# One load of B's sample rows moved to GpSimd's queue, beside two smaller reorderings, in a hybrid decoder step on one core

## The chip, the cores and the metric

The kernel is one program on 1 core of one Trainium2 chip. The metric is the device time of one execution in microseconds (us). A core has five engines that run side by side and meet through semaphores: TensorE (PE in the profile, its weight loads PEld), VectorE (DVE), ScalarE (ACT), GpSimd (POOL) and SyncE (SP), which issues most of the DMAs. ACT and POOL have DMA queues of their own. Each engine takes its instructions strictly in the order of its own program, so an instruction that waits holds all that stand behind it.

## The reference, cut to what matters

One layer of a decoder: 256 new prompt tokens and 8 samples of 8 tokens (320 tokens in all), width 2048, in float32.

```python
def decoder_layer(x, ssm_state, ssm_conv_state, ffn_conv_state, p):
    h = rms_norm(x, p["norm_mix_pre"])
    proj = h @ p["w_in"]                 # [gMLP u | gMLP v | SSD z | SSD x,B,C | dt]
    ...
    gate_out, chunk_v = chunk_spatial_gate(a_u, a_v, ...)     # gelu(u) * (tril(W_s) v_norm + b)
    ssm_out, new_ssm, new_ssm_conv = ssd_mixer(z, xbc, dt_raw, ssm_state, ...)
    mix = jnp.concatenate([gate_out, ssm_out], axis=-1) @ p["w_out"]
    x = x + rms_norm(mix, p["norm_mix_post"])
    f, new_ffn_conv = conv_ffn(rms_norm(x, p["norm_ffn_pre"]), ffn_conv_state, ...)
    return x + rms_norm(f, p["norm_ffn_post"]), new_ssm, new_ssm_conv, new_ffn_conv, chunk_v

# in ssd_mixer: convolution and silu over x, B, C, then for 4 groups of 8 heads
#   h_t = exp(dt_t a) h_{t-1} + dt_t x_t B_t^T,   y_t = h_t C_t
# y = (y + d_skip * x) * silu(z); y is normed over each group of 512 columns; * norm_w
```

The samples bring a recurrent state (8 samples, 32 heads, 64 x 128 each), which is read, decayed, added to and written back.

## The kernel before, in words

**Products.** Every large product is made in three matmuls: a weight slab of 512 KB is loaded in float32 (tile `wraw`, by SP), rounded by ACT (`whi`, line 123), the rest is taken by DVE (`wlo`, line 124), and PE adds high x high, low x high and high x low for all 320 tokens at a time (lines 153 to 155). `wraw`, `whi` and `wlo` have three buffers each, so a load starts when the `wlo` three slabs back is made, and a rounding when PE has left the `whi` three slabs back. One slab is 24 matmuls.

**Stages.** W_in's column blocks and W_out's row blocks take turns: v, B and C (their result for B, turned to rows of tokens, is written to `b_d` in DRAM by `to_tokens`), x of the first head group, four projections of u (`gate_up`), each followed by `gate_mix` and by a part of W_out (`chunk_out`), then the four SSD groups with x, z and W_out's other parts, then the feed-forward layer. The gate stage has its tiles in the pool `gp`, the SSD stage in the pool `sd`, which takes over `gp`'s memory: the first instruction that writes to an `sd` tile waits for the last readers of `gp`.

**Small work between slabs.** `ssd(g)`, `norm()` and others are generators. After each slab a `tick` lets them issue their next step; a `yield 24, 0` asks for 24 matmuls in between. What they issue is then laid into each engine's order by a scheduler that goes by priorities (`first()`, `tc.high_priority`) and by its own times. The order in which the program text issues things is therefore not the order of the engines.

**What the change touches.**
- `b4` (lines 838 to 841): B's 64 sample rows, 32 at a time, each block written four times under one another to 128 partitions. SP loads two tiles of 128 x 512 from `b_d`; the tiles lie in `sd`, under the tags `s1` and `xde`.
- `b_of_samples` (lines 843 to 848): ACT copies `b4` to `bsp` in another column order, rounded; for the partitions 32 to 63 and 96 to 127 DVE takes the rest. `picked` later scales `bsp` to `bm` on ACT.
- `norm` (lines 1136 to 1146): y times its root, four blocks, each split into a high (`ohi`) and a low part (`olo`) for `chunk_out`.
- `shrinks` (line 1054): the step at which GpSimd decays each of a group's pairs of states `st` (line 969).
- The tag `pv` of pool `tp` has four buffers; `scaled` (line 409) puts each block of a gate projection there (`ev`) before ACT's Gelu reads it.

PE's short work of a group, in this order: `xt_ps` (transposes of the samples' x), `s_ps`, then `yo_ps` (line 958), which reads the four pairs of states; the fourth pair, `st3`, is loaded last (line 883). `cs` (line 875) are rows of sums that the decays of the scores need.

Of the kernel before, what the change touches and what calls it, by code (L numbers as in the profile page):

```python
# [8 lines left out]
F32 = mybir.dt.float32  # L9
# [3 lines left out]
ALU = mybir.AluOpType  # L13
# [3 lines left out]
P = 128  # L17
NP = 256
NB, TS = 8, 8
NS = NB * TS  # L20
NT = NP + NS
# [12 lines left out]
def hybrid_step(  # L34
# [10 lines left out]
    act, dve, pool, pe, sp = nc.scalar, nc.vector, nc.gpsimd, nc.tensor, nc.sync  # L45
# [6 lines left out]
    tp = ctx.enter_context(tc.tile_pool(name="tp", bufs=2))  # L52
# [46 lines left out]
    def col(i):  # L99
        return prm[:, i:i + 1]  # L100


    def first():

        return tc.high_priority(offset=200000)
# [60 lines left out]
    def advance(tasks, task):  # L166

        try:
            need = next(task) or (0, 0)
            due[task] = made_so_far[0] + need[0], need[1]  # L170
            return True
        except StopIteration:
            tasks.remove(task)
            return False
# [13 lines left out]
    def finish(task):  # L188
        while task in side:
            advance(side, task)  # L190
        while task in bg:
            advance(bg, bg[0])
# [60 lines left out]
    def chunk_out(w, ck, hi, lo, begins, done=None, rate=1, apart=False):  # L253

        for nb in range(KD):
            if nb % 2 == 0:
                wb = slab(rows_of(w, 4 * ck, 4, P * nb, 256))
            ps = mm.tile([P, 512], F32, tag="mm", name=f"pd_{ck}_{nb}")
            for k in range(4):
                made = accumulate(ps[:, :NT], wb(k, nb % 2), hi[:, k, :], lo[:, k, :], k == 0, k == 3)  # L260
            with first():
                if begins:
                    act.copy(acc[:, nb, :], ps[:, :NT])
                else:
                    for ts in parts_of(nb) if apart else (slice(0, NT),):
                        added_last[:] = [dve.tensor_tensor(out=acc[:, nb, ts], in0=acc[:, nb, ts], in1=ps[:, ts], op=ALU.add).ins]  # L266
            if done is not None:
                done(nb)
            if nb % 2 == 1:
                for _ in range(rate):  # L270
                    tick()
        pd_last.append(made)
# [53 lines left out]
    def partial_sums(total, to):  # L326

        turned = tp.tile([P, NT], F32, tag="pv", name="turned", bufs=4)
        dve.transpose(out=turned, in_=total)
        small = tp.tile([P, NT], F32, tag="pv", name="small", bufs=4)  # L330
        part = small[:, 0:SN]
        dve.tensor_reduce(out=part, in_=turned.rearrange("p (s f) -> p s f", f=32), axis=mybir.AxisListType.X, op=ALU.add)
        sp.dma_start(to, part)
        return small
# [11 lines left out]
    def add_square(total, x, begins, adder=pool, place=("sq", 2)):  # L346
        if begins:
            act.activation(total, x, AF.Square)
        else:
            sq = tp.tile([P, NT], F32, tag=place[0], name="sq", bufs=place[1])  # L350
            act.activation(sq, x, AF.Square)
            adder.tensor_tensor(out=total, in0=total, in1=sq, op=ALU.add)
# [27 lines left out]
    b_d = dr.tile([NT, 512], F32, name="b_d")  # L380
# [26 lines left out]
    def scaled(ps, func, out):  # L407

        ev = tp.tile([P, NT], F32, tag="pv", name="ev", bufs=4)
        with first():  # L410
            dve.tensor_tensor(out=ev, in0=ps[:, :NT], in1=r1, op=ALU.mult)
        func_ins.append(act.activation(out, ev, func).ins)

    def split(hi, lo, x, scale=None):

        if scale is None:
            act.copy(hi, x)
            made = dve.tensor_tensor(out=lo, in0=x, in1=hi.bitcast(F32), op=ALU.subtract)
        else:
            high.append(act.activation(hi, x, AF.Copy, scale=scale).ins)  # L420
            made = dve.scalar_tensor_tensor(out=lo, in0=x, scalar=scale, in1=hi.bitcast(F32), op0=ALU.mult, op1=ALU.subtract)

        return made.ins

    def out_parts(pool_, name):
        return (pool_.tile([P, 4, NT], F32R, tag=f"{name}hi", name=f"{name}hi"),
                pool_.tile([P, 4, NT], F32R, tag=f"{name}lo", name=f"{name}lo"))
# [16 lines left out]
    def in_order(ap):  # L444

        return ap.rearrange("p (i j f) -> p j i f", j=4, f=32)
# [6 lines left out]
    with ExitStack() as mctx:  # L453
        op = mctx.enter_context(tc.tile_pool(name="op", bufs=1))
# [155 lines left out]
        with tc.tile_pool(name="gp", bufs=1) as gp:  # L610
# [60 lines left out]
            for n in range(2):  # L671
                ps = banks("ps_v")
                for kt in range(KD):
# [27 lines left out]
                    if n == 1 and kt == 4:  # L701
                        params()
                        for q in range(4):
                            rs = slice(32 * q, 32 * q + 32)
# [55 lines left out]
            def gate_up(g):  # L760
                uf = gp.tile([P, 4, NT], F32, tag="vf", name="uf", bufs=2)
                project(w_in, U0 + 512 * g, lambda j, ps: scaled(ps, AF.Gelu, uf[:, j, :]))
                return uf
# [52 lines left out]
            for g in range(4):  # L816
                res = []
                mix = gate_mix(g, uf, res)
                bg.append(mix)
                if g < 3:  # L820
                    uf = gate_up(g + 1)
                    finish(mix)
                    chunk_out(w_out, g, *res, g == 0)
            finish(mix)
# [3 lines left out]
        with tc.tile_pool(name="sd", bufs=1) as sd:  # L828
            btok = sd.tile([P, 2, 512], F32, name="btok")

            bsp = sd.tile([P, 2, 512], F32R, name="bsp")
# [3 lines left out]
            pool.tensor_copy(cb[NS:, NT:], ident[NS:, NS:])  # L835
            for c in range(2):
                act.copy(btok[:, c].rearrange("p (j i f) -> p j i f", j=4, f=32), in_order(b_raw[:, 512 * c:512 * c + 512]))
            b4 = [sd.tile([P, 512], F32, tag=tag, name="b4", bufs=n) for tag, n in (("s1", 1), ("xde", 2))]
            for i in range(2):
                o = NP + 32 * i  # L840
                sp.dma_start(b4[i], b_d[o:o + 32].unsqueeze(0).broadcast_to([4, 32, 512]))

            def b_of_samples():
                for i in range(2):
                    act.copy(bsp[:, i].rearrange("p (j i f) -> p j i f", j=4, f=32), in_order(b4[i]))
                    for rs in (slice(32, 64), slice(96, P)):
                        h = bsp[rs, i].rearrange("p (j i f) -> p j i f", j=4, f=32)
                        dve.tensor_tensor(out=h, in0=in_order(b4[i][rs]), in1=h.bitcast(F32), op=ALU.subtract)

            def load_state(g, i):  # L850

# [13 lines left out]
            def ssd(g):  # L865
# [63 lines left out]
                for r in range(2):  # L929
# [3 lines left out]
                                  in0=ps[:, :NP].rearrange("p (c t) -> p c t", c=2),  # L933
                                  in1=upper.unsqueeze(1).to_broadcast([P, 2, P]), op=ALU.mult)
                dve.tensor_tensor(out=cb[NS:, :NS], in0=ps[NS:, NP:NT], in1=upper_s[NS:], op=ALU.mult)
                dve.tensor_tensor(out=cb[:NS, NT:], in0=ps[:NS, NP:NT], in1=upper_s[:NS], op=ALU.mult)
                for hb in range(2):
                    dve.tensor_tensor(out=cms[:, 4 * hb:4 * hb + 4], in0=cmask[:, 4 * hb:4 * hb + 4],
                                      in1=cT[:, g, NP + 32 * hb:NP + 32 * hb + 32].unsqueeze(1).to_broadcast([P, 4, 32]),
                                      op=ALU.mult)  # L940
# [60 lines left out]
                s1 = sd.tile([P, 512], F32, tag="s1", name="s1", bufs=1)  # L1001
# [49 lines left out]
                                             op0=ALU.mult, op1=ALU.add)  # L1051
                ends = {2: 0, 5: 1, 7: 2, 10: 3}
                picks = {0: (0, 1), 2: (2,), 5: (3,)}
                shrinks = {0: 0, 3: 1, 5: 2, 8: 3}
                e = 1 if g == 3 else 0
                heads = {0: 0, 1: 1, 3: 2, 4: 3, 5: 4, 7: 5, 9 - e: 6, 10 - e: 7}
                states = {4: (g, 3), 7: (g + 1, 0), 9: (g + 1, 1), 12: (g + 1, 2)}
# [1 line left out]
                for n in range(13 - e):  # L1059
# [23 lines left out]
                    if n < 12 - e:  # L1083
# [4 lines left out]
                                   in1=dec[:, 2, h0:h0 + 8].unsqueeze(2).to_broadcast([P, 8, 64]), op=ALU.mult)  # L1088
# [32 lines left out]
            def heads_out(g):  # L1121

                ssq = hp.tile([P, NT], F32, tag="ssq", name="ssq")
                y = x_of.pop(g)

                def z_evac(j, ps):
                    while y_made.get(g, -1) < j:
                        advance(bg, bg[0])
                    zs = tp.tile([P, NT], F32, tag="ev", name="zs", bufs=2)
                    with first():  # L1130
                        scaled(ps, AF.Silu, zs)
                        dve.tensor_tensor(out=y[:, j, :], in0=y[:, j, :], in1=zs, op=ALU.mult)
                        add_square(ssq, y[:, j, :], j == 0, dve)
                project(w_in, Z0 + 512 * g, z_evac)

                def norm():
                    yield 24, 0
                    small = partial_sums(ssq, ssq_d[g])
                    yield 24, 0
                    rb = tp.tile([P, NT], F32, tag="pv", name="rb", bufs=4)  # L1140
                    root_by_vector(small, ssq_d[g], 1.0 / 512, rb)

                    res[g] += [h[:, KD - 4:] for h in hT] if g == 3 else out_parts(hp, "o")
                    for j in range(4):
                        dve.tensor_tensor(out=y[:, j, :], in0=y[:, j, :], in1=rb, op=ALU.mult)
                        split(res[g][0][:, j, :], res[g][1][:, j, :], y[:, j, :], col(prm_at["norm"][3] + 4 * g + j))
                task = norm()
                side.append(task)
                return task
# [97 lines left out]
    with tc.tile_pool(name="fp", bufs=1) as fp:  # L1247
# [157 lines left out]
        for k in BY_POOL:  # L1405
            f = acc[:, k, :]
# [111 lines left out]
```

## Time and profile before

| what | value |
|---|---|
| time, median of 3 runs | 1768.94 us (1768.35 to 1769.97) |
| time of the profiled execution | 1768.21 us |
| its span, first to last instruction | 1766.5 us |
| PE busy | 1754.9 us, 99% |
| DVE, ACT, POOL busy | 1171.0, 823.7, 286.4 us |
| granted TensorE clock | 0.999 |
| HBM | 167 GB/s over the span |

The 1.7 us between the profiled execution's time and its span lie outside the instructions. A matmul of 320 columns has a record of 0.31 us, while in an undisturbed row the next one starts about 0.147 us later: records overlap, so busy time hides short stalls. A stall is read from the starts of neighbouring matmuls in the timeline.

### The profile page before, as it was taken

What the parts mean: (1) busy time and instruction counts of PE and PEld (TensorE: products, weight loads), DVE (VectorE), ACT (ScalarE), POOL (GpSimd) and SP (SyncE); (2) the same over time, 40 slices, a digit from 0 to 9 for tenths busy, and PEclk for the clock granted to TensorE, in tenths of its full rate; (3) what the DMA queues carried; (4) which work ended last, traced back from release to release, by engine and by line L of the source; (5) the groups of instructions that cost most, each with busy time, mean ns of one, the idle gap of its engine ahead of it and who ended that gap; (6) DMA issues with size and microseconds to landing.
All of it is one profiled execution on the core that took longest, in us unless ns stands there. A gap on an engine that the chain in (4) does not pass through costs nothing.

```text
span 1766.5 us, 30627 instructions
## 1 busy us (share of the span) xinstructions
PE 1754.9 (99%) x11873; PEld 1708.2 (97%) x11873; DVE 1171.0 (66%) x2020; ACT 823.7 (47%) x1200; POOL 286.4 (16%) x627
## 2 busy tenths in 40 slices
PE   9999999999999999999999999999999999999998
PEld 7789999999899999999999999999999999999998
DVE  7549774656869777788855565665657565656575
ACT  5434555333655575655645434343434343333445
POOL 1202220000313222112211111010202010101004
PEclk9999999999999999999999999999999999999999
DMA  7556655455676766665654545554554545454542
GB/s 261 161 153 169 192 167 160 149 153 156 213 224 181 238 199 210 199 208 162 186 155 146 157 146 157 146 157 146 156 148 154 150 152 150 153 156 145 155 152 103
DMA packets 221051, 296.97 MB, mean 168 GB/s; under 512 B 19945, under 2 KB 147305, under 8 KB 220713
## 3 DMA queue, kind: packets, MB, share of 16 engines
q1 hardware_dynamic: 208568, 274.61, 51.5%
q10 hardware_dynamic: 9584, 13.38, 2.1%
q0 software_dynamic: 2752, 7.02, 1.4%
q8 instruction: 94, 1.54, 0.4%
q14 instruction: 53, 0.43, 0.1%
HBM read 277.88 MB, written 17.07 MB: 167 GB/s over the span
## 4 chain that ended last, share of the span: by engine, by line
PE 60%; DVE 0%; ACT 0%; issue 0%; ACTq 0%
PE ps L153 12%; PE ps L155 12%; PE ps L154 12%; PE pd L155 7%; PE pd L154 7%; PE pd L153 7%; PE x1p L1381 0%; PE fin_ps L1111 0%; PE y_ps L1039 0%; PE tsum L311 0%; PE ps_one L153 0%; PE ps_one L155 0%; PE ps_one L154 0%; PE ps_other L153 0%; PE ps_other L155 0%; PE ps_other L154 0%
## 5 line engine op out<-in xcount | busy, mean ns | idle before, releaser
L124 DVE TENSOR_TENSOR wlo<-wraw,whi 128x1024 fp32r<-128x1024 f32 (+1 forms) x476 | 582.6, 1224 | 427.0 <-ACT whi L123 424.7
L123 ACT CAST whi<-wraw 128x1024 fp32r<-128x1024 f32 (+1 forms) x475 | 494.7, 1042 | 676.2 <-PE ps L154 333.3
L153 PE MATMUL ps<-h_hi,whi 128*128 128x320 f32 x2268 | 700.7, 309 | 1.0 <-ACT whi L123 0.7
L155 PE MATMUL ps<-h_hi,wlo 128*128 128x320 f32 x2268 | 698.6, 308 | 0.7 <-DVE wlo L124 0.7
L154 PE MATMUL ps<-h_lo,whi 128*128 128x320 f32 x2268 | 699.1, 308 | 0.0
L153 PEld LDWEIGHTS ps<-h_hi,whi 128*128 128x128 f32 x2268 | 425.5, 188 | 4.1 <-issue 1.2
L155 PEld LDWEIGHTS ps<-h_hi,wlo 128*128 128x128 f32 x2268 | 425.5, 188 | 1.0 <-DVE wlo L124 1.0
L154 PEld LDWEIGHTS ps<-h_lo,whi 128*128 128x128 f32 x2268 | 425.7, 188 | 0.4
L155 PE MATMUL pd<-fhi,wlo 128*128 128x320 f32 x704 | 217.0, 308 | 0.0
L153 PE MATMUL pd<-fhi,whi 128*128 128x320 f32 x704 | 217.0, 308 | 0.0
L154 PE MATMUL pd<-flo,whi 128*128 128x320 f32 x704 | 217.0, 308 | 0.0
L153 PE MATMUL pd<-ohi,whi 128*128 128x320 f32 x448 | 138.9, 310 | 1.3 <-DVE pad L474 1.3
L155 PE MATMUL pd<-ohi,wlo 128*128 128x320 f32 x448 | 138.3, 309 | 0.0
L154 PE MATMUL pd<-olo,whi 128*128 128x320 f32 x448 | 138.3, 309 | 0.0
L153 PEld LDWEIGHTS pd<-fhi,whi 128*128 128x128 f32 x704 | 132.1, 188 | 0.0
L154 PEld LDWEIGHTS pd<-flo,whi 128*128 128x128 f32 x704 | 132.1, 188 | 0.0
L155 PEld LDWEIGHTS pd<-fhi,wlo 128*128 128x128 f32 x704 | 132.1, 188 | 0.0
L1283 POOL COPY ptf<-pad 128x2 f32<-128x2 f32 x88 | 21.0, 238 | 600.0 <-DVE pad L1271 599.4
L266 DVE TENSOR_TENSOR acc_ffn<-acc_ffn,pd 128x320 f32<-128x320 f32 (+1 forms) x161 | 77.5, 482 | 37.8 <-PE pd L155 36.4
L153 PEld LDWEIGHTS pd<-ohi,whi 128*128 128x128 f32 x448 | 84.1, 188 | 2.4 <-issue 1.3
L154 PEld LDWEIGHTS pd<-olo,whi 128*128 128x128 f32 x448 | 84.1, 188 | 0.3
L155 PEld LDWEIGHTS pd<-ohi,wlo 128*128 128x128 f32 x448 | 84.1, 188 | 0.0
(337 smaller groups left out, 1868.0 us busy)
## 6 DMA issues: line engine op xcount, KB each, us to landing
wraw<-in_ffn_w_up SPq DMA_DIRECT2D x176, 512.0 KB, 3.7
wraw<-in_w_in SPq DMA_DIRECT2D x140, 512.0 KB, 3.8
wraw<-in_ffn_w_down SPq DMA_DIRECT2D x88, 512.0 KB, 3.4
wraw<-in_w_out SPq DMA_DIRECT2D x64, 512.0 KB, 3.4
st<-in_state_ssm SPq DMA_DIRECT2D x40, 256.0 KB, 4.8
out_ssm_state_sample<-st ACTq DMA_DIRECT2D x30, 256.0 KB, 2.6
cs<-dacs_d SPq DMA_DIRECT2D x16, 320.0 KB, 5.1
xr<-in_xT SPq DMA_DIRECT2D x4, 640.0 KB, 4.1
```

The costliest lines, as they stand in the source:

```text
L123: rounded[:] = [act.copy(hi, raw).ins]
L124: dve.tensor_tensor(out=lo, in0=raw, in1=hi.bitcast(F32), op=ALU.subtract)
L153: pe.matmul(ps, whi, xhi, start=first, stop=False)
L154: pe.matmul(ps, whi, xlo, start=False, stop=False)
L155: last_made[0] = pe.matmul(ps, wlo, xhi, start=False, stop=last).ins
L266: added_last[:] = [dve.tensor_tensor(out=acc[:, nb, ts], in0=acc[:, nb, ts], in1=ps[:, ts], op=ALU.add).ins]
L1283: pool.tensor_copy(ptf[:, k, :], pad[:, 256:258])
```

## The change

Three edits. First, `b4` becomes four tiles of 128 x 256 in `tp`'s four `pv` buffers; they are asked for when the last gate projection (`gate_up(3)`) has been issued, and GpSimd's queue loads them. `b_of_samples` works on four halves where there were two tiles. Second, `norm` yields once after its second block. Third, the second pair of states is decayed at step 2 and not at step 3.

```diff
@@ -819,6 +819,12 @@
                 if g < 3:
                     uf = gate_up(g + 1)
+                    if g == 2:
+                        b4 = [[tp.tile([P, NT], F32, tag="pv", name="b4", bufs=4)[:, :256] for _ in range(2)] for _ in range(2)]
+                        for i in range(2):
+                            o = NP + 32 * i
+                            for h in range(2):
+                                pool.dma_start(b4[i][h], b_d[o:o + 32, 256 * h:256 * h + 256].unsqueeze(0).broadcast_to([4, 32, 256]))
                     finish(mix)
                     chunk_out(w_out, g, *res, g == 0)
@@ -835,17 +841,14 @@
-            b4 = [sd.tile([P, 512], F32, tag=tag, name="b4", bufs=n) for tag, n in (("s1", 1), ("xde", 2))]
-            for i in range(2):
-                o = NP + 32 * i
-                sp.dma_start(b4[i], b_d[o:o + 32].unsqueeze(0).broadcast_to([4, 32, 512]))
-
             def b_of_samples():
                 for i in range(2):
-                    act.copy(bsp[:, i].rearrange("p (j i f) -> p j i f", j=4, f=32), in_order(b4[i]))
-                    for rs in (slice(32, 64), slice(96, P)):
-                        h = bsp[rs, i].rearrange("p (j i f) -> p j i f", j=4, f=32)
-                        dve.tensor_tensor(out=h, in0=in_order(b4[i][rs]), in1=h.bitcast(F32), op=ALU.subtract)
+                    for h in range(2):
+                        out = bsp[:, i].rearrange("p (j i f) -> p j i f", j=4, f=32)[:, :, 2 * h:2 * h + 2]
+                        raw = in_order(b4[i][h])
+                        act.copy(out, raw)
+                        for rs in (slice(32, 64), slice(96, P)):
+                            dve.tensor_tensor(out=out[rs], in0=raw[rs], in1=out[rs].bitcast(F32), op=ALU.subtract)
@@ -1051,7 +1054,7 @@
-                shrinks = {0: 0, 3: 1, 5: 2, 8: 3}
+                shrinks = {0: 0, 2: 1, 5: 2, 8: 3}
@@ -1144,6 +1147,8 @@
                         split(res[g][0][:, j, :], res[g][1][:, j, :], y[:, j, :], col(prm_at["norm"][3] + 4 * g + j))
+                        if j == 1:
+                            yield 24, 0
```

What this does to the engines' orders, at three places; line numbers are those of each program. SP's queue at the start of the first SSD group, first before, then after the change (`b_4210`, `b_4211` are the two tiles `b4`; `st_4261` and its like are `st3`):

```order
L841 DMA b_4210<-b_d 128x1x512
L841 DMA b_4211<-b_d 128x1x512
L117 DMA wraw<-in_w_in 128x4x256
L854 DMA st<-in_state_ssm 128x512 x5
L117 DMA wraw<-in_w_in 128x4x256
L854 DMA st<-in_state_ssm 128x512
L883 DMA st_4261<-in_state_ssm 128x512
L117 DMA wraw<-in_w_out 128x4x256
L883 DMA st_4262<-in_state_ssm 128x512
L875 DMA cs<-dacs_d 128x2x320
```

After the change:

```order
L857 DMA st<-in_state_ssm 128x512 x2
L117 DMA wraw<-in_w_in 128x4x256
L857 DMA st<-in_state_ssm 128x512 x4
L117 DMA wraw<-in_w_in 128x4x256
L886 DMA st_4265<-in_state_ssm 128x512
L886 DMA st_4266<-in_state_ssm 128x512
L878 DMA cs<-dacs_d 128x2x320
L117 DMA wraw<-in_w_out 128x4x256 x3
```

The two `b4` loads are gone from SP; two states stand ahead of the first slab, and both `st3` and the first `cs` ahead of the third.

ACT's order at the same place, before the change (`btok` is B of the prompt, `x_4267` the samples' x, `b_4210` and `b_4211` again `b4`):

```order
L837 COPY btok<-b_raw 128x512 x2
L450 COPY x_4267<-xs 128x512 x2
L845 COPY bsp<-b_4210 128x512
L845 COPY bsp<-b_4211 128x512
L123 COPY whi<-wraw 128x1024 x2
L963 ACTIVATE bm<-bsp,bsel 128x256 x2
L123 COPY whi<-wraw 128x1024 x2
L1018 ACT_TABLE_LOAD
L1018 ACTIVATE cpx<-cs 128x256
```

After the change (`b_3874` to `b_3877` are the four halves):

```order
L843 COPY btok<-b_raw 128x512 x2
L450 COPY x_4271<-xs 128x512 x2
L849 COPY bsp<-b_3874 128x4x64
L849 COPY bsp<-b_3875 128x4x64
L849 COPY bsp<-b_3876 128x4x64
L849 COPY bsp<-b_3877 128x4x64
L123 COPY whi<-wraw 128x1024 x2
L966 ACTIVATE bm<-bsp,bsel 128x256 x2
L123 COPY whi<-wraw 128x1024
L1021 ACT_TABLE_LOAD
L1021 ACTIVATE cpx<-cs 128x256
```

The copies of `b4` stand where they stood, ahead of the next two roundings of weights; one rounding has moved behind the first `cpx`.

GpSimd's order from the last loads of `gate_mix`, before the change:

```order
L770 DMA wT<-in_gate_wT 128x512
L772 DMA bs<-in_gate_b_s 128x512
L897 TENSOR_TENSOR xde<-xdt,dec 128x512
L969 TENSOR_TENSOR st<-st,tote 128x512 x6
L1019 TENSOR_TENSOR cpx<-cpx,cT 128x256
L897 TENSOR_TENSOR xde<-xdt,dec 128x512
```

After the change:

```order
L772 DMA bs<-in_gate_b_s 128x512
L827 DMA b_3874<-b_d 128x1x256
L827 DMA b_3875<-b_d 128x1x256
L827 DMA b_3876<-b_d 128x1x256
L827 DMA b_3877<-b_d 128x1x256
L900 TENSOR_TENSOR xde<-xdt,dec 128x512
L1022 TENSOR_TENSOR cpx<-cpx,cT 128x256
L972 TENSOR_TENSOR st<-st,tote 128x512 x6
```

Four loads have come in, and in the first group `cpx` now stands ahead of the six decays. All orders outside this stretch, and PE's order everywhere, are the same in both programs. A program with the edit of `norm` alone and one with the edit of `shrinks` alone have, engine by engine, the order of the kernel before.

## The prediction

> **What bounds the kernel now.** I read the page first, then the waits of PE, then PE's timeline where they lie, and from there backwards: ACT, SP, the DMA engines.
>
> ```profile
> PE 1754.9 (99%) x11873; PEld 1708.2 (97%) x11873; DVE 1171.0 (66%) x2020; ACT 823.7 (47%) x1200; POOL 286.4 (16%) x627
> ...
> PE yo_ps L958 <- DMA st<-in_state_ssm: 1.5, 1, 1.5
> PE pd L153 <- DVE pad L474: 1.3, 2, 1.1
> ...
> PE ps L155 <- DVE wlo L124: 0.7, 1, 0.7
> PE ps L153 <- ACT whi L123: 0.7, 1, 0.7
> ```
>
> PE is the bound, and PE's program is the same after the change. So only PE's stalls can be won, and only new ones lost. The waits name 1.5, 0.7 and 0.7 us at one place, the start of the first SSD group. That is 2.9 us of idle records; since records overlap, the loss itself is read from starts:
>
> ```profile
> 440.04 0.31 PE L154 MATMUL ps<-h_lo,whi 128*128 128x320 f32 x1
> 440.19 0.31 PE L155 MATMUL ps<-h_hi,wlo 128*128 128x320 f32 x1
> 441.16 0.42 PE L153 MATMUL ps<-h_hi,whi 128*128 128x320 f32 x1 [0.66 <-ACT whi L123]
> ...
> 442.42 0.42 PE L155 MATMUL ps<-h_hi,wlo 128*128 128x320 f32 x1 [0.70 <-DVE wlo L124]
> 442.67 0.31 PE L153 MATMUL ps<-h_hi,whi 128*128 128x320 f32 x1
> ...
> 445.75 1.04 PE L433 MATMUL xt_ps<-ident,x 128*128 128x128 f32 x8
> 447.58 2.10 PE L958 MATMUL yo_ps<-st,cb_cms 128*32 128x256 f32 x26
> 451.70 0.41 PE L153 MATMUL ps<-h_hi,whi 128*128 128x320 f32 x1
> ```
>
> Starts lie 0.147 us apart (440.04 to 440.19, rounded). From 440.19 to 442.67 there are four steps: 2.48 us in place of 0.59, so 1.89 us lost. For the short work after it, the second group is the measure, where nothing waits:
>
> ```profile
> 529.64 1.03 PE L433 MATMUL xt_ps<-ident,x 128*128 128x128 f32 x8
> 531.47 1.93 PE L958 MATMUL yo_ps<-st,cb_cms 128*32 128x256 f32 x32
> 533.33 0.41 PE L153 MATMUL ps<-h_hi,whi 128*128 128x320 f32 x1
> ```
>
> There it takes 533.33 - 529.64 = 3.69 us, here 451.70 - 445.75 = 5.95: another 2.26 us lost. Together 4.15 us. Now what PE waits for, on ACT and on SP's queue:
>
> ```profile
> 434.99 0.62 ACT L845 CAST bsp<-b 128x512 fp32r<-128x512 f32 x1 [3.05 <-DMA b<-b_d]
> 439.54 0.62 ACT L845 CAST bsp<-b 128x512 fp32r<-128x512 f32 x1 [3.93 <-DMA b<-b_d]
> 440.06 1.99 ACT L123 CAST whi<-wraw 128x1024 fp32r<-128x1024 f32 x2
> ...
> 428.75 1.24 SPq L841 DMA_DIRECT2D b<-b_d  x2
> 430.42 0.38 SPq L117 DMA_DIRECT2D wraw<-in_w_in  x1
> ...
> 442.39 0.38 SPq L117 DMA_DIRECT2D wraw<-in_w_in  x1
> ...
> 443.36 0.43 SPq L883 DMA_DIRECT2D st<-in_state_ssm  x1
> ...
> 445.49 0.50 SPq L883 DMA_DIRECT2D st<-in_state_ssm  x1
> ```
>
> ACT stands 3.05 + 3.93 us for `b4`, issued only at 428.75, and the two roundings behind it come at 440.06: that is the first stall. The roundings free no `wraw` meanwhile, so SP's next slab goes at 442.39 and `st3` behind it at 443.36 and 445.49: that is the second. The transfers themselves are slow:
>
> ```profile
> DMA  8593000022399999999999322225699999998999
> GB/s 67 179 413 118 0 0 0 30 27 100 109 214 269 215 234 243 249 209 222 216 235 370 132 100 97 97 100 79 177 322 398 414 370 370 376 312 237 245 275 355
> ...
> st<-in_state_ssm SPq DMA_DIRECT2D x8, 256.0 KB, 10.7
> ...
> wraw<-in_w_in SPq DMA_DIRECT2D x2, 512.0 KB, 10.3
> ...
> wraw<-in_w_out SPq DMA_DIRECT2D x6, 512.0 KB, 3.4
> ```
>
> The first two rows cut 425 to 452 us into 40 slices of 0.675. Behind `b4` (430.4 to 432.4) and again from 439.9 to 443.2 only 2 or 3 tenths of the 16 DMA engines are busy, at 97 to 132 GB/s, where full slices move up to 414. A transfer that lies on four engines looks like that; 256 KB at 100 GB/s take 2.6 us, both tiles 5.2. What lies behind them in the same queue lands 10.3 to 10.7 us after its issue; the last row, of 385 to 425 us, has 3.4 for a slab. The Trainium skill ("DMA: Bandwidth & Descriptors", Why a DMA increments its semaphore by 16 and not by 1) says that a transfer is split over the largest number of engines up to 16 that divides its slowest dimension. Here that is the 4 of the fourfold rows, and the trace agrees with its quarter of the engines; the rule speaks against the new loads as well, whose slowest dimension is still 4.
>
> **The change part by part.**
>
> *Loads moved.* The `pv` buffers come free when ACT's last Gelu has read `ev`, and the loads follow:
>
> ```profile
> 394.68 0.47 ACT L412 ACTIVATE uf<-ev 128x320 f32<-128x320 f32 x1
> DMA to landing us min/median/max: 1.8/2.9/4.0
> ...
> 432.03 1.04 POOL L897 TENSOR_TENSOR xde<-xdt,dec 128x512 f32<-128x512 f32 x1 [49.58 <-ACT x L450]
> ```
>
> The second row is of the transfers that touch `b_d`, most of them on GpSimd's queue. So the last half goes at about 395.2 and lands by 399; with the slowest of today's landings (10.7) by 406. It is needed when ACT gets to it, at 434.99 - 3.05 = 431.94. At least 25 us of cover. Behind the four issues on GpSimd stands `xde`, which waits for ACT until 432 anyhow (third row); the next users of `pv` are the z projections, far behind. The moved loads cost nothing.
>
> *ACT and DVE after it.* Four copies of 128 x 256 and eight subtractions of 32 x 256 take the place of two and four. Nearest rows:
>
> ```profile
> 452.28 0.42 ACT L1018 ACTIVATE cpx<-cs 128x256 f32<-128x256 f32 x1 [3.33 <-DMA cs<-dacs_d]
> 449.54 0.42 DVE L892 TENSOR_TENSOR xdt<-xt_ps,dt 32x256 f32<-32x256 f32 x1
> ```
>
> ACT: 4 x 0.42 = 1.7 us from 431.94, so to 433.6 (as two copies of 0.62: 433.2). PE has work until 440.33 (440.19 and one step) and leaves the `whi` buffer that the first rounding needs two slabs earlier: 440.33 - 2 x 3.52 = 433.3. So that rounding is made at 433.6 to 434.7 and its `wlo` by 436: over 4 us ahead of PE, where today it is 0.9 late. The second has 3.5 us more of PE's time before it. DVE: 8 x 0.42 = 3.4 us, three ahead of the first `wlo`, five behind it; they feed `bm`, which PE reads long after. I take nothing for either, because the 4 us hide both ends.
>
> *SP after it.* The first `wlo` by 436 frees `wraw`, so the slab now issued at 442.39 goes at about 436 and both `st3` at 436.5 to 437. With today's 10.7 they land at 447.7, with twice the undisturbed 3.4 at 443.8. PE begins `yo_ps` 1.89 us earlier, at 445.7, and gets to its fourth pair after three quarters of 1.9 us, at 447.1. I take the landing without `b4` in the queue, since full slices above show 370 to 414 GB/s: second stall gone. The other end, 0.6 us of it left, stays for the range.
>
> *Order of decays.* `cpx` ahead of the six decays in the first group: it waits for `cs`, which is now issued about 9 us earlier too; the decays wait for `yo_ps` in any case. Nothing.
>
> *`norm` and `shrinks`.* Each alone moves no row on any engine. The wait of 1.3 us on `pad` in the second group, to which `norm`'s splits on DVE belong, therefore stays.
>
> Sum on the profiled execution: 1768.21 - 4.15 = 1764.06. That execution lies 0.73 below the median, 1768.94; carried to the median: **1764.8**, 0.23% less. About 0.2%, 3.54 us, is what a measurement of this kernel can tell from no change, so below 1765.40 is faster and above 1772.48 slower. The forecast stands only 0.6 us beyond that line.
>
> **The rivals.**
>
> *DVE becomes late instead.* Freed of its wait for data, DVE's chain of the first group runs beside the six decays. In the second group it does so already:
>
> ```profile
> 532.20 8.01 POOL L969 TENSOR_TENSOR st<-st,tote 128x512 f32<-128x512 f32 x6 [11.15 <-PE yo_ps L958]
> 539.46 1.96 DVE L938 TENSOR_TENSOR cb_cms<-cmask,cT 128x128 f32<-128x128 f32 x2
> 541.34 1.76 DVE L124 TENSOR_TENSOR wlo<-wraw,whi 128x1024 fp32r<-128x1024 f32 x1
> ```
>
> From `xt_ps` to the end of that `wlo` are 543.10 - 529.64 = 13.5 us. Counted from 443.9 (445.75 - 1.89) the like `wlo` ends at 457.3; PE needs it 3.69 us and three slabs after 443.9, at 458.1. The cover is 0.8 us. If it fails, the price is a wait like that on `pad`, up to 1.3: 1766.1. For it: the thin cover. Against: the second group lives with the like cover, and the waits of PE name none there. The Trainium skill ("SBUF — State Buffer", SBUF: two separate sides) has DVE and GpSimd exclude each other for a whole instruction when DVE reads two SBUF inputs and GpSimd reads SBUF. By it each such DVE instruction could wait up to a decay, 8.01 / 6 = 1.3 us, and one more of these would use the cover up; the 1.96 us for two small products are in line with it.
>
> *The loads of `st` are held up by themselves.* Full slices between 432 and 439 move only 209 to 269 GB/s; if that is the doing of the `st` loads and not `b4`'s, the second stall stays and only 1.89 us are won: 1767.1. Against it: 370 to 414 later, with `st` in the queue too.
>
> *The new loads hold the weights up (slower).* Near 395 the four halves, 5.2 us on four engines by the rate above, share these with the slabs.
>
> ```profile
> 396.06 7.41 SPq L117 DMA_DIRECT2D wraw<-in_w_out  x3
> ...
> 404.25 1.05 ACT L123 CAST whi<-wraw 128x1024 fp32r<-128x1024 f32 x1 [2.43 <-PE pd L154]
> ```
>
> The load of 396.06 is rounded at 404.25, three slabs on, and PE needs it two slabs later, at 411.3. With 3.4 us to land and 2.3 for rounding and `wlo` it may be 9.5 us late. `b4` made a slab 6.9 us late (10.3 against 3.4), so the cover holds. Beyond it PE waits: if the first late slab also delays the next on ACT, each costs up to 6.9 over the forecast, 1771.7 for one and 1778.6 for two.
>
> *More is won.* If `norm`'s wait should go with the shift, 1.3 more: 1763.5.
>
> **How the numbers follow.** Forecast 0.62, of which 0.12 is put within 0.2%, because the three runs spread over 1.6 us and the line is 0.6 away; its own range is 1763.9 to 1765.7. DVE late 0.15, `st` held up 0.10, weights held up 0.08 (half of it as one slab, half as two), more won 0.05. Faster: 0.50 + 0.05 = 0.55. Slower by over 0.2%: 0.04. Within: the rest, 0.41. The range leaves out the slower rival and takes in the others: 1763.2 to 1767.3.
>
> **What would show it.** Right: no ACT wait on `b`, PE without a stall at 440, the short work of the first group 3.7 us as in the second, slabs near 430 landing within 6 us, everything later about 4.15 us earlier with the waits on `pad` as they are. A wait of PE on `wlo` near 458 is the first rival, on `st` near 447 the second, on `whi` or `wlo` near 400 the third. Wrong altogether would be a stall at a place that none of these names.

## The result, and the profile after

The kernel after takes 1764.57 us (median of 9 runs, 1764.0 to 1767.23), the kernel before, on the same chip, 1768.35 (9 runs, 1767.0 to 1770.57): a ratio of 0.998, 95% interval 0.9971 to 0.9989, or 3.8 us less. The profiled execution took 1764.57 us with a span of 1762.9 (before: 1768.21 and 1766.5). Its rows, in the order of those of before; first PE's waits (total, times, longest):

```profile
PE ps_v L143 <- ACT h_hi L639: 0.4, 1, 0.4
...
PE pd L154 <- DVE h_lo L421: 0.2, 1, 0.2
PE pd L153 <- DVE pad L474: 0.2, 1, 0.2
```

The waits on `st`, `wlo` and `whi` are gone, and so, against the prediction, is the 1.1 us on `pad` (DVE's copy of a finished product out of `ps`, for which PE waits before its next product); 0.2 us are left there. PE's timeline at the two stalls:

```profile
440.22 0.31 PE L155 MATMUL ps<-h_hi,wlo 128*128 128x320 f32 x1
440.37 0.31 PE L153 MATMUL ps<-h_hi,whi 128*128 128x320 f32 x1
...
443.88 1.03 PE L433 MATMUL xt_ps<-ident,x 128*128 128x128 f32 x8
...
445.71 1.93 PE L961 MATMUL yo_ps<-st,cb_cms 128*32 128x256 f32 x32
447.57 0.41 PE L153 MATMUL ps<-h_hi,whi 128*128 128x320 f32 x1
```

The products go through at 0.147 us, and the short work takes 447.57 - 443.88 = 3.69 us, as in the second group. What fed it, on ACT, DVE and SP's queue:

```profile
431.88 1.32 ACT L849 CAST bsp<-b 128x256 fp32r<-128x256 f32 x4
433.42 1.05 ACT L123 CAST whi<-wraw 128x1024 fp32r<-128x1024 f32 x1 [0.22 <-ACT bsp L849]
...
434.57 1.23 DVE L124 TENSOR_TENSOR wlo<-wraw,whi 128x1024 fp32r<-128x1024 f32 x1
...
435.83 0.38 SPq L117 DMA_DIRECT2D wraw<-in_w_in  x1
436.25 0.98 SPq L886 DMA_DIRECT2D st<-in_state_ssm  x2
```

ACT finds `b4` there and waits for nothing; the rounding comes at 433.42, its `wlo` ends at 435.80, and SP's slab and both halves of `st3` go within 1.5 us of that. The DMA engines in the same window of 425 to 452 us, and the new loads:

```profile
DMA  7693000897597899996799999996894001996586
...
st<-in_state_ssm SPq DMA_DIRECT2D x8, 256.0 KB, 5.6
...
wraw<-in_w_in SPq DMA_DIRECT2D x2, 512.0 KB, 5.3
```
```profile
390.23 0.71 POOL L827 DMA_DIRECT2D b<-b_d  x1 [7.75 <-ACT uf L412]
...
395.48 0.68 POOL L827 DMA_DIRECT2D b<-b_d  x1 [1.05 <-ACT uf L412]
```

From issue to landing these four take:

```profile
DMA to landing us min/median/max: 3.8/4.3/5.1
```

No run of 2s and 3s is left; `st` lands in 5.6 us in place of 10.7. PE runs the same 11873 products in both kernels, so their starts can be subtracted one by one. PE's start in a kernel less that in the profile of before, in us, just ahead of the first group and behind it, behind the second group's `pad`, in the third group, behind the last norm and at the last product (worked out from the traces):

```
              436    452    575    700    790   last
after        0.03  -4.13  -5.28  -5.24  -4.54  -3.83
after_again -0.05  -4.21  -5.19  -4.98  -4.86  -4.95
load_only    0.08  -4.08  -3.83   0.21   0.26   0.19
two_edits    0.45   0.95   0.91   1.00   1.14   1.04
plain_rows   0.13  -4.03  -3.86  -3.37  -2.95  -2.26
late_reader  0.15  -3.05  -3.49  -3.29  -2.26  -1.46
sp_queue     0.08  -4.08  -3.24  -2.75  -2.12  -2.22
sp_four     11.23   7.07   6.83   8.27   8.79   8.69
no_decay     0.45  -3.71  -4.93  -5.12  -4.81  -4.91
mults_first -0.06  -4.22  -4.04  -2.30  -2.31  -2.40
```

So the first group won 4.16 us, the second 1.15 more, and 1.45 were given back by the last product: 0.7 around 782 and 0.8 at the very end. The other rows are the experiments. One of the 11 executions of `load_only` took 7638 us, with no profile to say why; without it the median of that run would be 0.1 us lower.

### The profile page after: what moved, and what is told of

It reads as the page before. It is cut to its first block, busy times and chain, and to the rows that moved or that the text cites. A ratio compares the mean times of both kernels' runs of the same rounds, so it can differ in the third digit from the quotient of the medians.

```text
span 1762.9 us, 30639 instructions
## 1 busy us (share of the span) xinstructions
PE 1754.5 (100%) x11873; PEld 1708.9 (97%) x11873; DVE 1172.7 (67%) x2024; ACT 824.7 (47%) x1202; POOL 292.2 (17%) x631
## 4 chain that ended last, share of the span: by engine, by line
PE 59%; DVE 1%; DMA 0%; issue 0%; ACT 0%; SPq 0%; DVEq 0%; ACTq 0%
PE ps L153 12%; PE ps L155 12%; PE ps L154 12%; PE pd L154 6%; PE pd L155 6%; PE pd L153 6%; DVE wlo L124 0%; PE x1p L1386 0%; DMA small<-ssq_d 0%; PE fin_ps L1114 0%; DVE acc_mix L266 0%; DMA ssq_d<-small 0%; PE tsum L311 0%; PE y_ps L1042 0%; PE ps_one L153 0%
```

## The experiments

Two theories stood against each other on the cause. Mine: the loads come late, and ACT's order lets them hold the roundings. The rival: what holds `st` and the weights is the backlog of the four engines themselves.

**Which edit does it.** `two_edits` keeps `norm`'s extra step and the earlier decay alone; `load_only` the loads alone:

```diff
 two_edits (on before)
-                shrinks = {0: 0, 3: 1, 5: 2, 8: 3}
+                shrinks = {0: 0, 2: 1, 5: 2, 8: 3}
 ...
+                        if j == 1:
+                            yield 24, 0
```

> The kernel before with norm's extra step and the earlier decay, and without the new loads. Every engine has the same instructions in the same order with the same waits as before, so my theory expects the time of before, 1768.4 us (within 1.6), with stalls of 1.9 and 2.3 us near 440 and 451. What is open is the wait on pad near 559.8: if it belongs to the program, it is again 1.1 to 1.3 us; if it hangs on when the transfers of st happen to land (GpSimd's two decays of st3 at 555.3 lie beside DVE's splits there), it may differ from run to run. A rival by which these two edits won part of the gain expects 1 us or more less than before.

> The kernel after without norm's extra step and the earlier decay; the same order of instructions on every engine as after. My theory: all the gain, so 1764.6 us, and no wait of PE on whi, wlo or st at 440 to 452. The two places where the profile of after gave something back are read here again: the wait on h_lo at 782 (0.6 us), which should stay if the chain of the third group's norm sets it, and the granted clock of 0.52 from 1749 to 1752 (about 0.7 us), which should be gone or elsewhere if it is chance. The rival (the three edits work together) expects over 1766.

`two_edits`: 1769.22 us, ratio 1.0004 (0.9995 to 1.0013): nothing. Both stalls are in its profile again; the wait on `st` is only 0.4 us, since the products ahead of it took 1.5 us longer, at a granted clock of 0.51 from 444.0 to 447.2. `load_only`: 1765.06, ratio 0.9983 (0.9974 to 0.9992), with no stall at 440 to 452 and 4.16 us won there, as in after. So the gain is the loads'. The profiled execution of `load_only` was one of its longest, 1768.55, and shows how a later place can give all of it back: 4 us are lost in the third group, 640 to 700. There the norm's partial sums make a trip through DRAM, and the last of the four 5 KB loads stands in SP's queue behind a slab, as it does in after:

```profile
636.11 0.38 SPq L117 DMA_DIRECT2D wraw<-in_w_in  x1
637.23 1.29 SPq L341 DMA_DIRECT2D small<-ssq_d  x3
638.61 0.40 SPq L117 DMA_DIRECT2D wraw<-in_w_out  x1
639.05 0.51 SPq L341 DMA_DIRECT2D small<-ssq_d  x1
...
646.15 0.23 DVE L342 TENSOR_REDUCE small<-small 128x10 f32<-128x40 f32 x1 [5.08 <-DMA small<-ssq_d]
...
687.72 1.28 ACT L1021 ACT_TABLE_LOAD   x1 [7.45 <-DMA cs<-dacs_d]
```

The transfers of that trip, from issue to landing:

```profile
DMA to landing us min/median/max: 3.8/4.4/7.1
```

In after the longest of them is 4.3, not 7.1 us; why the same order landed so late here is open. DVE stands 5.08 us for it, in after 0.55, and its later work, `pad` among it, is late for PE: 2.5 of the 4 us, at 656 and 663. The other 1.5 come near 693, where DVE's `wlo` and `acc_mix` (its sum of W_out's products) are late behind ACT, which had stood 7.45 us for `cs` (the last row; in after 6.01).

**ACT's order or the engines' backlog.** `late_reader` leaves the loads as they were and puts ACT's copies behind the first of the two roundings:

```diff
-                if g == 0:
-                    yield 48, 0
-                    with tc.issue_after(last_made[0]):
-                        b_of_samples()
                 yield 48, 72
+                if g == 0:
+                    with tc.issue_after(last_made[0]), tc.issue_after(rounded[-1]):
+                        b_of_samples()
```

> The kernel before with its loads as they were (four engines, SP's queue, issued at 428.75), but with ACT's two copies of b4 and DVE's subtractions behind one of the two roundings that stood behind them. If the order on ACT is what matters (my theory), the first rounding comes at about 433.5 and its wlo by 436, SP's next slab at about 436 and both st3 by 437.5; the second rounding, behind the copy that waits to 440.2, is done by 441.3 and PE needs it at 443.9. Then both stalls go: 4.1 us less on the span, 1764.3 to 1764.9. If the four engines' backlog holds what is behind b4 in the queue (the rival), st lands as late as before and the second stall of 2.3 us stays: 1766.5. The slices with 2 or 3 tenths of the DMA engines busy stay in either case.

1766.42 us, ratio 0.9986 (0.9977 to 0.9994). 3.20 of the 4.16 us are won in the first group. ACT's timeline, one row of DVE's, then SP's queue and the DMA engines:

```profile
433.54 1.05 ACT L123 CAST whi<-wraw 128x1024 fp32r<-128x1024 f32 x1 [1.45 <-issue]
434.50 0.62 ACT L845 CAST bsp<-b 128x512 fp32r<-128x512 f32 x1
438.52 0.62 ACT L845 CAST bsp<-b 128x512 fp32r<-128x512 f32 x1 [3.40 <-DMA b<-b_d]
439.04 1.05 ACT L123 CAST whi<-wraw 128x1024 fp32r<-128x1024 f32 x1
...
440.58 1.23 DVE L124 TENSOR_TENSOR wlo<-wraw,whi 128x1024 fp32r<-128x1024 f32 x1
...
436.30 2.54 SPq L854 DMA_DIRECT2D st<-in_state_ssm  x2
439.81 0.33 SPq L883 DMA_DIRECT2D st<-in_state_ssm  x1
441.84 0.38 SPq L117 DMA_DIRECT2D wraw<-in_w_out  x1
442.26 0.50 SPq L883 DMA_DIRECT2D st<-in_state_ssm  x1
```
```profile
DMA  6594000022259999999999999859998779979899
...
st<-in_state_ssm SPq DMA_DIRECT2D x8, 256.0 KB, 9.5
```

The copy still waits 3.40 us for `b4`, but PE's first stall is gone. About 1 us stays in the products with `st`: the second half of `st3` goes at 442.26, later than the 437.5 that I expected, and PE's last six products start at 448.09, 5.8 us after that. The 9.5 us is the median of eight loads of `st`; it isn't what holds this half. The slab of 441.84 ahead of it waits for the second rounding's `wlo`, which ends at 441.81, and that rounding stands behind the second copy of `b4`. So the order on ACT is the first stall and over half of the second, and part of the rest as well, since one rounding was left behind a copy that waits; how much is the backlog in the queue this run doesn't tell.

**The four engines themselves.** `plain_rows` keeps the place, the issues and the bytes of the two loads and changes their shape. It leaves out the right data: each load reads 128 other rows of `b_d` in place of 32 of the samples' rows four times:

```diff
-                sp.dma_start(b4[i], b_d[o:o + 32].unsqueeze(0).broadcast_to([4, 32, 512]))
+                sp.dma_start(b4[i], b_d[P * i:P * i + P])
```

> The kernel before in which the two loads of b4 read 128 plain rows of the same tensor each, in place of 32 rows four times: the same bytes, issues, places and order, but a slowest dimension of 128 in place of 4. The sample rows of B are thus replaced by other rows. If the four engines are what makes the loads slow, b4 lands 3.4 to 5 us after its issue, ACT's waits of 3.05 and 3.93 us shrink to under 2 us together, no slice from 430 to 443 has 2 or 3 tenths, and both stalls go: about 1764.6. If the place in the queue is what matters (behind it 256 KB loads of st, ahead of it slabs), the waits stay over 4 us together and the first stall stays at 1 us or more: 1766 to 1768.

1764.6 us, ratio 0.9981 (0.9972 to 0.999), and 4.16 us won in the first group: all of it, with the loads at the old place in the old queue. ACT, and the DMA engines from 425 to 452 us:

```profile
431.98 1.14 ACT L845 CAST bsp<-b 128x512 fp32r<-128x512 f32 x2
433.52 1.05 ACT L123 CAST whi<-wraw 128x1024 fp32r<-128x1024 f32 x1 [0.41 <-ACT bsp L845]
```
```profile
DMA  6694000799598899999999999998999315996987
...
b<-b_d SPq DMA_DIRECT2D x2, 256.0 KB, 2.8
```

As many bytes land in 2.8 us, and ACT waits for nothing. So the old place costs nothing when the shape is another; either edit alone, of the place or of the shape, takes both stalls away. The Trainium skill's rule of the slowest dimension ("DMA: Bandwidth & Descriptors", Why a DMA increments its semaphore by 16 and not by 1) gives 16 engines for 128 rows and 4 for four times 32, and these two runs agree.

`by_rows` asks whether the right data can have that shape where they are, as four loads of 32 rows each:

```diff
-                sp.dma_start(b4[i], b_d[o:o + 32].unsqueeze(0).broadcast_to([4, 32, 512]))
+                for q in range(4):
+                    sp.dma_start(b4[i][32 * q:32 * q + 32], b_d[o:o + 32])
```

> The kernel before, with each of its two loads of b4 as four loads of 32 rows (the same right data, a slowest dimension of 32 in place of 4, eight issues in place of two) at the old place on SP's queue. The planner answers by another order there: one rounding ahead of each copy, six more issues ahead of the loads of st, and products of slabs between those with st on TensorE. By my theory (only the four engines made the loads late) ACT waits for b less than 1 us and the first stall of 1.9 us goes; the second goes too if st, now issued later, still lands ahead of its products. Then 1764.6. If it does not, 1 to 3 us stay: 1766 to 1768. The rival (it has to be off SP's queue) expects 1768 or more.

1768.28 us, ratio 1.0 (0.9991 to 1.0009): nothing won. The samples' rows are read four times over as in before, now as eight loads of 64 KB that land in 3.4 us (last row, median), so it isn't the repeated reading that made the loads slow. ACT's two copies wait 0.70 us in all and the first stall is gone, but that is not the shape's doing alone: one rounding now stands ahead of each copy, and in `late_reader` a rounding ahead of the copies removed that stall by itself. On SP six more issues of `b4` and a slab that goes only at 435.64 now stand ahead of the loads of `st`, whose first goes at 437.09 (before: 430.85), and PE's longest wait is for them:

```profile
435.64 0.39 SPq L117 DMA_DIRECT2D wraw<-in_w_in  x1
436.08 0.97 SPq L842 DMA_DIRECT2D b<-b_d  x2
437.09 0.42 SPq L855 DMA_DIRECT2D st<-in_state_ssm  x1
...
449.24 0.63 PE L959 MATMUL yo_ps<-st,cb_cms 128*32 128x256 f32 x6 [1.80 <-DMA st<-in_state_ssm]
...
b<-b_d SPq DMA_DIRECT2D x8, 64.0 KB, 3.4
```

It lies between my two cases: reshaping the loads in this way, with the orders that come with it, wins nothing; moving them does.

**The third rival's price.** `sp_queue` issues the new loads from SP, ahead of the slab of 396; `sp_four` makes each round four times, one round ahead of each of four slabs (`for _ in range(4):` around the load):

```diff
-                                pool.dma_start(b4[i][h], b_d[o:o + 32, 256 * h:256 * h + 256].unsqueeze(0).broadcast_to([4, 32, 256]))
+                                sp.dma_start(b4[i][h], b_d[o:o + 32, 256 * h:256 * h + 256].unsqueeze(0).broadcast_to([4, 32, 256]))
```

> The kernel after, with the four new loads issued by SP, at the same place, behind the fifth of the eight slabs there. This asks whether GpSimd's queue is needed. SP has to wait for the same buffers (390 to 395 us) and the slabs stand behind that wait, so the slab of about 396 may be issued a few us later and lands behind four loads on four engines (5.2 us). The prediction's cover for such a slab is 9.5 us, so my theory expects no wait of PE near 400 to 412 and the time of after, 1764.6 us. The rival (third rival of the prediction) expects a wait on whi or wlo there of 1 to 7 us: 1766 to 1772.

> As the kernel after with the loads on SP, but each round of four loads made four times into the same buffers, one round ahead of each of four slabs. It prices the third rival. A round waits for the landing of the one before it, some 5 to 7 us, in place of the 3.5 us from slab to slab; over four slabs the slabs fall 6 to 14 us behind, against a cover of 9.5 us. If the cover is right, PE waits on whi or wlo between 405 and 425 for as much as a slab is later than 9.5 us, and nowhere before: 0 to 5 us, 1764.6 to 1770. If the cover is much smaller than reckoned (4 us), the loss is over 8 us.

`sp_queue`: 1764.69 us, ratio 0.9977 (0.9968 to 0.9986). Its slab is issued at 396.14 and the rounding waits for its landing until 404.63, 8.5 us: 5.1 later than the undisturbed 3.4, and PE notices nothing. GpSimd's queue isn't needed. `sp_four`: 1774.59 us, ratio 1.0039 (1.0025 to 1.0052). ACT:

```profile
404.84 1.05 ACT L123 CAST whi<-wraw 128x1024 fp32r<-128x1024 f32 x1 [2.99 <-DMA wraw<-in_w_out]
412.52 1.05 ACT L123 CAST whi<-wraw 128x1024 fp32r<-128x1024 f32 x1 [6.63 <-DMA wraw<-in_w_out]
420.09 1.04 ACT L123 CAST whi<-wraw 128x1024 fp32r<-128x1024 f32 x1 [6.51 <-DMA wraw<-in_w_out]
```

The second is made at 407.85 in `sp_queue`. Here it is 4.7 us late, and PE's first loss is 0.6 us (at 415.37). Its slab was issued at 403.90, 4.3 us later than in after, and landed 8.6 after that, 5.2 late: together 9.5, of which 0.6 showed. The cover was 8.9; I had reckoned 9.5. Beyond it PE waits: it is 11.2 us behind at 436, more than the 0 to 5 I expected. Some 4.6 of these are waits behind slabs, which went at 7.6 us from each other, not 3.5; 2.4 are waits near 436 and 438 on DVE, which is late because the slabs of the next projection fell late as well. The other 4.2 are no waits: the granted clock was 0.50 from 423.0 to 428.7 and 0.51 from 440.0 to 442.5, and PE's steps there were 0.267 us in place of 0.147. This profile is of the longest of four executions, 1777.14 us. The 4.16 us of the first group were won even so.

**The wait on `pad`.** `no_decay` leaves out the two products on GpSimd that decay each group's fourth state:

```diff
-                    if n in shrinks:
+                    if n in shrinks and n != 8:
```

> The kernel after without the decay of each group's fourth state of the samples (two products of 128 x 512 on GpSimd per group; these states are thus left undecayed). The profiles of before and of three other kernels have a wait of 1.0 to 1.2 us of PE on pad in the second group, with DVE's splits and wlo beside these two products stretched from 1.93 to 2.74 and from 1.22 to 2.08 us; after has none there. If the two engines' exclusion makes that wait (my theory), there is none over 0.3 us here, the four splits take 1.93 us and the wlo 1.22, and the time is that of after or up to 1.2 us less: 1763.4 to 1764.6. If the wait has another source, it comes back in this profile or in the spread of the times.

1763.36 us, ratio 0.9973 (0.9964 to 0.9983). Of DVE's timeline, before, after and `no_decay` in turn (its splits and the `wlo` behind them), with GpSimd's products above the first two:

```profile
555.32 2.74 POOL L969 TENSOR_TENSOR st<-st,tote 128x512 f32<-128x512 f32 x2 [13.30 <-DMA st<-in_state_ssm]
...
554.39 2.74 DVE L421 SCALAR_TENSOR_TENSOR olo<-xs,prm,ohi 128x320 fp32r<-128x320 f32 x4
557.06 2.08 DVE L124 TENSOR_TENSOR wlo<-wraw,whi 128x1024 fp32r<-128x1024 f32 x1
```
```profile
552.18 3.09 POOL L972 TENSOR_TENSOR st<-st,tote 128x512 f32<-128x512 f32 x2 [14.25 <-DMA st<-in_state_ssm]
...
550.26 1.93 DVE L421 SCALAR_TENSOR_TENSOR olo<-xs,prm,ohi 128x320 fp32r<-128x320 f32 x4
552.12 1.22 DVE L124 TENSOR_TENSOR wlo<-wraw,whi 128x1024 fp32r<-128x1024 f32 x1
```
```profile
551.15 1.93 DVE L421 SCALAR_TENSOR_TENSOR olo<-xs,prm,ohi 128x320 fp32r<-128x320 f32 x4
553.00 1.22 DVE L124 TENSOR_TENSOR wlo<-wraw,whi 128x1024 fp32r<-128x1024 f32 x1
```

In before the products begin 0.93 us into the splits, as soon as `st` lands, and DVE takes 0.81 + 0.86 us more; in after they begin 1.92 us after them, when the `wlo` has just begun, and it is GpSimd that takes longer. Without them DVE is undisturbed, and PE has no wait on `pad` that the profile lists. That is the exclusion which the Trainium skill states ("SBUF — State Buffer", SBUF: two separate sides). These rows give it a price: 1.7 us of DVE, 1.2 of PE at this place (-3.88 to -5.09 in after's starts). Which of the two engines waits hangs on when `st` lands: of ten profiles with these products in this order, seven show the stretched splits (before, `two_edits`, `load_only`, `plain_rows`, `sp_queue`, `sp_four`, `mults_first`) and three do not (after, `after_again`, `late_reader`). In the seven the products begin 0.9 to 1.35 us into the splits, in the three 1.38 to 1.92. The median of `no_decay` is 1.2 to 1.8 us below those of the five runs with after's loads; the intervals overlap, so the traces carry this, not the times.

**The late norm.** `mults_first` puts the four multiplications of the last group's norm ahead of its splits:

```diff
+                    for j in range(4 if g == 3 else 0):
+                        dve.tensor_tensor(out=y[:, j, :], in0=y[:, j, :], in1=rb, op=ALU.mult)
                     for j in range(4):
-                        dve.tensor_tensor(out=y[:, j, :], in0=y[:, j, :], in1=rb, op=ALU.mult)
+                        if g < 3:
+                            dve.tensor_tensor(out=y[:, j, :], in0=y[:, j, :], in1=rb, op=ALU.mult)
```

> The kernel after with the four multiplications of the last group's norm ahead of its splits, in place of one ahead of each split. In after PE waited 0.6 us at 782 for the last h_lo, which DVE made late because its multiplication stood behind a wlo. With the multiplications first the last h_lo is ready over 1 us before PE needs it, the wait goes, and the span is 0.6 us shorter: about 1764.0 in the median, which the times can't tell from after; the trace can. The rival: the chain over DRAM ahead of it is late anyway, and the wait moves to an earlier h_lo.

1764.99 us, ratio 0.998 (0.9971 to 0.9989). The loss around 782 is gone (-2.30 at 700, -2.31 at 790), but one profile doesn't show that the edit did it: with the old order the loss was no more than 0.05 to 0.14 us in `load_only`, `after_again` and `two_edits` too. The time is that of after. The profile, of an execution of 1765.96, lost 1.7 us between 575 and 700 to waits on `pad` and `acc_mix`. It is the one candidate for a better version that I ran; it can't be told from after.

**After once more.**

> The kernel after, once more, for its spread. 1764.6 within 1 us in the median. The wait of 1.1 us on pad in the second group, the late norm near 690 or 782 and a lowered granted clock near 1750 should come or go one by one, as chance; the 4.1 us at 440 to 452 should be won again.

1765.15 us, ratio 0.9979 (0.997 to 0.9988). This profile, span 1761.7, keeps 4.95 us to the last product.

## Why the prediction was right

The forecast, 1764.8, lies 0.2 us from the median and within the spread of repeats, but the exact hit owes something to chance: the sum had one term, and the profile has four.

- *The two stalls, 4.15 us.* Right: 4.16 in after, and 4.16 between 436 and 452 in every other profile with the early loads, `sp_four` among them. Step for step: first rounding at 433.6, measured 433.42; `wlo` by 436, measured 435.80; slab at 436, measured 435.83; `st3` by 437, measured 437.2 for the end of both issues.
- *The cause of them.* Incomplete. I had ACT's order as the cause and the four engines as why the loads were slow, and `plain_rows` shows that taking the second away is enough: the same order on ACT then costs nothing. What I expected of the shape for the moved loads, that the rule speaks against them too, did not matter: they are slow (4.3 us for 128 KB) where nobody waits.
- *Costs put at nothing.* Right. ACT's four copies took 1.32 us in place of 1.7, DVE's eight subtractions 1.30 + 2.15 = 3.45 where 3.4 was reckoned. The loads went at 390.23 to 395.48 (I had spoken of the last one) and landed within 5.1 us, 31 us ahead.
- *`norm` and the earlier decay do nothing.* Right (`two_edits`).
- *"The wait of 1.3 us on `pad` therefore stays."* This step failed. The same order of instructions is not the same wait: it hangs on the landing of `st`, and went in after. It was in the fourth rival, 0.05, as a consequence of the shift; in the runs it went in three of ten.
- *DVE late beside the decays.* It didn't fail: `wlo` ends at 457.11 (reckoned 457.3), 1.0 us ahead of the need at 458.1. The products on GpSimd took 7.78 us beside it, and it was stretched to 1.76.
- *Left out.* What comes behind the second group: the late last `h_lo` (the low part of the last norm's split; 0.7 us in after), the late trip through DRAM and the late `cs` (2.5 and 1.5 us in the profile of `load_only`), and the granted clock at the end (0.8 us). The prediction named "everything later about 4.15 us earlier"; at the last product it is between 5.0 earlier and 0.2 later in the profiles of after, `after_again` and `load_only`.

What stays open: why the clock is lowered in some runs, and how often the norm's trip is late; both were seen, not provoked. That the cover of 1.0 us at 458 would cost PE once it fails wasn't tried.

## What to carry to other kernels

Look at the shape of a load before its place: one whose slowest dimension is 4 took the queue's next transfers from about 5 to over 10 us, and a stall behind it on ACT and another on SP came from that one number. Where the shape is needed, issue it where nobody waits for it (here 31 us ahead of its reader; GpSimd's queue and SP's did equally well), and not as many small loads ahead of urgent ones, unless the orders that come of it are looked at. And a stall of a microsecond between two engines that exclude each other is a matter of phase: it is neither kept nor removed by leaving the order alone, so compare such kernels over several profiles.

## What the runs showed of the hardware that I had not expected

The granted clock falls for a few us in some executions. After, near its end, in a stretch (busy time of PE, PEld, DVE, ACT, POOL, then clock, DMA share and GB/s), and `after_again` for the same stretch:

```profile
1749.00:1752.00 3.00, 3.00 (x12) 2.61 (x11) 2.96 (x8) 0.72 (x2) 1.85 (x3) 0.52 0.15 55
```
```profile
1749.00:1752.00 3.00, 2.94 (x15) 2.07 (x14) 2.97 (x8) 0.68 (x3) 2.56 (x3) 1.00 0.29 104
```

A clock of 0.52 for about 3 us costs 0.8 us; `late_reader` and `plain_rows` have the like (0.61 over 3.5 us), the seven others of the table not at this place, with the same program on PE. Two of these seven have it elsewhere: `two_edits` (0.51 from 444.0 to 447.2, just behind PE's first stall, which before has without it) and `sp_four` (0.50 from 423.0 to 428.7, behind a wait of 3.8 us, and 0.51 from 440.0 to 442.5, behind one of 1.4).

And GpSimd took 0.68 to 0.71 us to issue one of the new loads, where SP issued two loads of `st` in 0.82.
